# MLA scores with a 128-row last product, and a down projection in 512-column matmuls

## The chip, the cores and the metric

One core of a Trainium2 chip. The time is what the device takes for one execution of the program, in microseconds (us), the median of several runs. Inputs and outputs lie in the device's memory (HBM).

## The reference

A backbone of two layers over 512 latent tokens and 256 context tokens, 1024 features, float32. Layer 1 mixes tokens by multi-head latent attention (MLA), layer 2 by a bidirectional gated recurrence. After each comes a SwiGLU feed-forward network with 2816 inner features. RMSNorm with a shift, a scale and a gate from the conditioning vector (adaLN) stands around each part. The parts that matter here:

```
# MLA: 8 heads; a query and a key have 128 own features and 64 rotary ones, and the rotary key is shared by all heads
q = concat([q_nope, q_rope])               # 128 + 64
k = concat([k_nope, broadcast(k_rope)])    # 128 + 64
s = einsum('bhqd,bhkd->bhqk', q, k) * scale
p = softmax(s);  o = p @ v                 # latent queries see all 768 keys, context queries the 256 context keys

# feed-forward
y = (silu(a @ w1) * (a @ w3)) @ w2         # w2: 2816 -> 1024, the down projection
x = x + gate * y
```

Layer 2 computes the latent tokens alone, so its down projection is 1024 x 2816 by 2816 x 512.

## The kernel before

**Numbers in two parts.** TensorE (PE) multiplies in float32r, which keeps fewer bits than float32. Each operand is cut into a high part (a cast on ScalarE, ACT) and a low part (the rest, a subtraction on VectorE, DVE, or on GpSimd, POOL). A product is then three matmuls: high by high, high by low, low by high. `mm3` (L93 to L99) issues them for a list of terms into one PSUM output, so L97, L98 and L99 are the lines of most matmuls. A matmul is written (rows * columns of the stationary operand) and the columns of the moving operand: `128*128 128x512`.

**The order of the work.** The program is written as a flow of operations on tiles. A planner orders them on each engine by priorities and by costs and due times of its own, and puts in the semaphores. `self.at(name)` marks a part with a priority. On the chip each engine runs its list in that order; a tile pool with `bufs=n` has n places for a tag, and an operation that writes a tile waits until the place is free.

**The attention** (`mla_attend`, L427 on). For each of 8 heads, products from the latent vectors are normalised, rotated, transposed (L489) and cut (L490 to L492) into `qk_hi` and `qk_lo`. Slot 0 holds the query's own features, slot 1 the key's, and slot 2 of `qk_hi` the rotary query: its high part on partitions 0 to 63, its low part on partitions 64 to 127. The rotary keys were made before the attention, in the loop over the six token tiles at the end of `mla_in`: `rope` delivers them in both halves of a tile, so `kr_hh` (L421) has the high part twice, and `kr_lo` (L423) the low part in partitions 0 to 63 alone. A head has six query blocks of 128 queries; four (latent) take 768 keys in chunks of 512 and 256 columns, two (context) take one chunk of 256 columns. A chunk is five matmuls into one PSUM output, L514 to L518: own features high by high, high by low, low by high; rotary features against `kr_hh` over 128 rows, which adds both parts of the query; and the rotary query's high part against `kr_lo` over 64 rows. Then DVE takes the maximum of a row (`nm`, L521), ACT the exponential (L524), DVE the reciprocal of the sum and the product with it (L526, L527), PE transposes the probabilities (L530), ACT and DVE cut them (L532, L533), and `mm3` multiplies with the values. Between these PE runs the next head's projections and products for the adaLN vectors (L158, tiles of 32 columns).

**The down projection** (`ffn_down`, L758 on). The inner features come in 11 pairs of 128. In layer 2 the first six pairs' values stay on chip in two parts (`gk`); the other five are stored to HBM and loaded again (L771) and cut (`gs`, L628 and L629). For each of eight output tiles c, three weight tiles are loaded on the queue of SyncE (L82), cast on ACT (L83) and subtracted on POOL (L84), in a ring of three places, and give 22 terms. `proj_out` makes one PSUM output for each segment of tokens that it gets, one after the other, and `residual` (L557) adds it to x with the gate. Layer 1 is called with `SEGS` (512 latent and 256 context tokens), layer 2 with `HALF` (twice 256 latent tokens). `po` takes the PSUM place by width: 512 columns from `big()`, which goes round the tags L (two places) and M (one), 256 columns from the tag q (five places). The products of the up projection before it use all eight. Each finished tile of layer 2 goes to the output at once (L788).

Of the kernel before, what the change touches and what calls it, by code (L numbers as in the profile page):

```python
# [10 lines left out]
F32 = mybir.dt.float32  # L11
# [6 lines left out]
P = 128  # L18
D = 1024
# [36 lines left out]
class Kernel:  # L56
# [14 lines left out]
    # ---- weights: float32 from DRAM, cut on chip into two float32r parts whose sum is exact  # L71
    def weight(self, name, idx, c0, c1, place=None):
        """columns c0:c1 of tile idx of a weight; a tile that was fetched ahead is handed out"""
        nc = self.nc
        key = (name, idx, c0, c1)
        if key in self.ahead:
            return self.ahead.pop(key)
        src, n = self.a[name][(*idx, slice(None), slice(c0, c1))], c1 - c0
        w = self.ring.tile([P, RING], F32, tag="wf", name="wf", bufs=4)
        with self.at("w"):  # L80
            hi, lo = place or (self.ring.tile([P, RING], F32R, tag=t, name=t, bufs=3) for t in ("wh", "wl"))
            nc.sync.dma_start(out=w[:, :n], in_=src)  # L82
            nc.scalar.copy(hi[:, :n], w[:, :n])  # L83
            nc.gpsimd.tensor_sub(lo[:, :n], w[:, :n], hi[:, :n].bitcast(F32))  # L84
        return hi, lo
# [7 lines left out]
    def mm3(self, out, terms):  # L93
        """out = sum over terms of (lhs_hi + lhs_lo)^T (rhs_hi + rhs_lo) but for lo lo."""
        nc, n = self.nc, len(terms)
        for i, ((lh, ll), (rh, rl)) in enumerate(terms):
            nc.tensor.matmul(out, lhsT=lh, rhs=rh, start=(i == 0), stop=False)  # L97
            nc.tensor.matmul(out, lhsT=lh, rhs=rl, start=False, stop=False)  # L98
            nc.tensor.matmul(out, lhsT=ll, rhs=rh, start=False, stop=(i == n - 1))  # L99

    def mm3m(self, outs):
        """mm3 of several outputs, their terms taken in turn"""
        nc = self.nc
        n = len(outs[0][1])
        for i in range(n):
            for out, terms in outs:
                (lh, ll), (rh, rl) = terms[i]
                nc.tensor.matmul(out, lhsT=lh, rhs=rh, start=(i == 0), stop=False)
                nc.tensor.matmul(out, lhsT=lh, rhs=rl, start=False, stop=False)
                nc.tensor.matmul(out, lhsT=ll, rhs=rh, start=False, stop=(i == n - 1))  # L110
# [38 lines left out]
    # ---- adaLN vectors: n chunks of 128 outputs (n <= 4), both streams  # L149
# [20 lines left out]
    def norm_scale(self, l, which, ks=range(KD)):  # L170
        """w * (1 + scale): [P, KD, 2]"""
        nc = self.nc
        m0 = 8 if which == 0 else 32
        k0, n = ks[0], len(ks)
        if k0 == 0:
            self.nsc[(l, which)] = self.const.tile([P, KD, 2], F32, name=f"nsc{l}{which}")
        v0 = (VEC_N1 if which == 0 else VEC_N2) + l * KD + k0
        w = self.vec[:, v0:v0 + n].unsqueeze(2).broadcast_to([P, n, 2])
        nc.vector.scalar_tensor_tensor(self.nsc[(l, which)][:, k0:k0 + n], self.mod[l][:, m0 + k0:m0 + k0 + n, :], 1.0, w,
                                       op0=ALU.add, op1=ALU.mult)  # L180

    # ---- RMSNorm over features of x (feature-major), modulated, cut in two parts
# [13 lines left out]
    def norm_rb(self, acc, segs, pool, rb, nt):  # L196
        """1/rms of every token, on all partitions, for each segment, from the sums of squares plus D * eps"""
        nc = self.nc
        rs, rbs = [], []
        for i, (s, c0, c1) in enumerate(segs):  # L200
            n = c1 - c0
            t4 = n // P
            tp = nt()
            for t in range(t4):
                nc.tensor.transpose(tp[:, t * P:(t + 1) * P], acc[:, c0 + t * P:c0 + (t + 1) * P], self.ident)
            r = pool.tile([P, 2, LT], F32, tag=f"nr{i}", name="nr", bufs=1)
            rs.append((r, t4))
            nc.vector.tensor_reduce(r[:, 0, :t4], tp[:, :n].rearrange("p (t f) -> p t f", f=P), axis=AX.X, op=ALU.add)
            nc.gpsimd.tensor_tensor(r[:, 1, :t4], r[:, 0, :t4], self.half.broadcast_to([P, t4]), op=ALU.pow)
        for i, (r, t4) in enumerate(rs):  # L210
            dg = pool.tile([P, LT, P], F32, tag="dg", name="dg", bufs=2)
            nc.vector.tensor_tensor(dg[:, :t4], self.ident.unsqueeze(1).broadcast_to([P, t4, P]),
                                    r[:, 1, :t4].unsqueeze(2).broadcast_to([P, t4, P]), op=ALU.mult)
            o = rb(i, *segs[i][1:])
            nc.tensor.matmul(o, lhsT=self.ones, rhs=dg[:, :t4].rearrange("p t f -> p (t f)"), start=True, stop=True)
            rbs.append(o)
        return rbs

    def norm(self, l, which, x, rbs, segs, pool, a_hi, a_lo, ks=range(KD)):
        """x: the streams, feature-major"""  # L220
# [13 lines left out]
    # ---- 1/sqrt(v + eps) of small tiles, with one Newton step  # L234
# [15 lines left out]
    def rope(self, out, m, tab, pool):  # L250
        """out [P, t, 128] (both halves alike) = m*tab0 + swap(m)*tab1, m [P, t, 64]"""
# [72 lines left out]
    def mla_in(self, es, mla, a_hi, a_lo):  # L324
# [9 lines left out]
        with ExitStack() as es1:  # L334
# [13 lines left out]
            # half of the features after the other: their shifts and scales, the normed streams, the projection's weights  # L348
# [12 lines left out]
        # tables  # L361
# [19 lines left out]
        # latent projections, token-major  # L381

        def proj(ts):
            """the first tokens' products go feature tile by feature tile, as the norm delivers them"""
# [14 lines left out]
        for t in range(TT):  # L399
# [23 lines left out]
            nc.vector.tensor_sub(kr_lo[0:64, ts], tp[0:64, 5, :], kr_hh[0:64, ts].bitcast(F32))  # L423
# [3 lines left out]
    def mla_attend(self, es):  # L427
        """the heads' outputs in two parts, and the first products of them for the latent tokens"""
# [9 lines left out]
        for h in range(H):  # L438
            # queries of two heads at once; a pair's columns: k0 and k1 of the queries, k2 and keys/values, keys/values
# [12 lines left out]
            for t0 in range(0, TT, BT):  # L452
                with self.at("m_proj"):
# [14 lines left out]
                    # columns of raw: q nope 128, q rope 64, k nope 128  # L468
# [24 lines left out]
            if h == H - 1:  # L493
                # in the place of what no head needs any more
# [5 lines left out]
            with self.at("m_att" if h < H - 1 else "m_last"):  # L500
                for q0, nq, k0, k1 in ((0, 2, 0, TT), (2, 2, 0, TT), (4, 2, 4, TT)):
# [3 lines left out]
                    for qi in range(nq):  # L505
                        qs = slice((q0 + qi) * P, (q0 + qi + 1) * P)
                        sc = ps.tile([P, NT], F32, tag="sc", name="sc")
                        for c0, c1 in ((0, 512), (512, 768)):
# [9 lines left out]
                            mm(o, lhsT=qk_hi[0:64, 2, qs], rhs=kr_lo[0:64, cs], start=False, stop=True)  # L518
# [32 lines left out]
    def residual(self, x, k, pos, gate, segs, pool=None, acc=None):  # L551
        """x[k] += gate * pos, and the squares of the new x[k] into acc"""
# [49 lines left out]
    # ---- products by Strassen and Winograd's scheme: seven for a 2 x 2 of blocks, rows by columns by tokens  # L602
    def strassen_weights(self, raw, w, fs, on_dve):
        """raw: the two rows' blocks [A11 A12], [A21 A22] of w columns each. Generator of (hi, lo) of the seven
        operands in the order of use: A11, A12, S2, S1, S3, S4, A22"""
# [25 lines left out]
    def ffn(self, es, l, x, segs, acc, ps, spool=None, acc1=None):  # L631
# [10 lines left out]
        with ExitStack() as es2:  # L642
            fs = self.pool(es2, "fs")
            fop = self.pool(es2, "fop")
            # parts hi, lo of the token blocks B11, B21, B22, T1, T3, T4, T2 of features k, k + 4; B12 is in T1's place at first
# [7 lines left out]
            # T1 until it may be written: in the place of what the first pair gives  # L653
# [43 lines left out]
    def strassen_tokens(self, y, T1):  # L697
        """y: token blocks B11, B12, B21, B22, the last three replaced by T3, T4, T2"""
# [10 lines left out]
    def ffn_first(self, l, p, hn, ops, fs, ps, st):  # L709
        """a pair of feature tiles block by block, as the norm delivers the operands"""  # L710
# [47 lines left out]
    def ffn_down(self, es, l, x, segs, n, gk, gd, ps, spool, acc):  # L758
# [4 lines left out]
        for p0, p1 in chunks:  # L763
# [14 lines left out]
            for c in range(KD):  # L778
# [5 lines left out]
                with self.at("d_mm"):  # L784
                    po = self.proj_out(ps, terms, segs)
                    self.residual(x, c, po, self.mod[l][:, 40 + c, :], segs, spool if last else None, acc if last else None)
# [3 lines left out]
    def lower_bounds(self):  # L790
        """softmax of lb_logits over the two layers: p1 is this layer's bound, p0 = 1 - p1; columns [dir, head]"""
# [16 lines left out]
    def layer1(self, es, x, f_hi, f_lo, es_act):  # L808
        nc, a = self.nc, self.a
        with ExitStack() as es1:  # L810
# [4 lines left out]
            with ExitStack() as es3:  # L815
# [12 lines left out]
                # products of the heads at hand while the last one is under way  # L828
# [50 lines left out]
    def hproj(self, h, m, ps, a_hi, a_lo, segs, turn=False):  # L879
        """feature-major projection m of head h, one PSUM tile for each token segment"""  # L880
# [11 lines left out]
    def head_proj(self, h, a_hi, a_lo, hp, tmp, ps):  # L892
        nc = self.nc
        # X slots: q fb.., kf, kb, q ff..; F: f by direction (backward, forward)
# [33 lines left out]
    def head(self, h, ih, pr, oT, tmp, ps, msk, zero, won):  # L928
        nc = self.nc
        X, F, Fc, Kc, q, k0, gs = pr  # L930
        # context: keys decayed to the context's end (forward) and to its start (backward)
# [15 lines left out]
        # levels inside the blocks of 32  # L947
# [3 lines left out]
        for l in range(6):  # L951
            L = 0 if l == 0 else 1 << (l - 1)
            if l:
                # keys of even blocks run forward, of odd blocks backward; the queries the other way
# [16 lines left out]
        # blocks of 32 and 64 in a tile of 128  # L971
# [23 lines left out]
        # states at the tiles' edges  # L995
# [14 lines left out]
        # readout  # L1010
# [23 lines left out]
    def grow(self, X, T, L, tmp):  # L1034
        """From blocks of L tokens to blocks of 2L: decays of the neighbour block onto queries and keys."""
# [13 lines left out]
def pack(i):  # L1049
    """The inputs in the layouts that the kernel loads; nothing but copies."""  # L1050
    f = {k: np.asarray(v) for k, v in i.items()}

    def cols(w, n):
        """[K, n*c] -> [c, 128, K/128 * n]"""
# [27 lines left out]
    # which pairs of a block of 32 tokens meet at which level: of shapes alone  # L1082
# [3 lines left out]
    # rotary tables: of the grid's shape alone  # L1086
# [25 lines left out]
```

## Time and profile before

| | |
|---|---|
| median of 3 runs | 1897.63 us (1892.61 to 1898.05) |
| profiled execution, first to last instruction | 1898.5 us |
| its time beside the span | not listed; the runs above are other executions |
| PE busy | 1799.4 us, 95% |
| PE weight loads (PEld) busy | 1619.9 us, 85% |
| DVE, ACT, POOL busy | 1127.1, 719.3, 840.6 us |
| DMA | 188.90 MB, mean 100 GB/s |

A matmul is pipelined: its length in the profile holds its way through the array, and the next one starts long before its end. So what a matmul costs in a full stream is the distance between the starts of two neighbours, and the sum of the lengths says little.

### The profile page before, as it was taken

The page shows a single profiled execution, that of the slowest core. Times are in us where ns is not written, and L with a number is a line of the kernel's source. Part 1 is how long each engine was busy: PE and PEld are TensorE (multiplying, and loading weights), DVE is VectorE, ACT ScalarE, POOL GpSimd, SP SyncE. Part 2 cuts the span into 40 slices and gives each one's busy share as a digit, 9 for nine tenths or more (in the row PEclk, how much of TensorE's full clock was granted, in tenths as well). Part 3 has the DMA queues.
Part 4 walks back from the last instruction along what each step waited for, and adds up shares of the span by engine and source line. Part 5 has one row for each costly group of instructions (what it writes and reads, how often), then busy time and mean ns, then how long its engine had stood idle before and what let it go on. Part 6 is the DMA issues. An engine that isn't in the chain of part 4 may idle for free. (4 is left out here: it accounts for less than half of the span.)

```text
span 1898.5 us, 34179 instructions
## 1 busy us (share of the span) xinstructions
PE 1799.4 (95%) x14170; PEld 1619.9 (85%) x14170; DVE 1127.1 (59%) x1733; ACT 719.3 (38%) x1347; POOL 840.6 (44%) x568
## 2 busy tenths in 40 slices
PE   5889999999999999999999999999998899999999
PEld 3878888778799999988887889888886689899999
DVE  5566786751667777643203666565654389999400
ACT  4354555542453333332212333323232454443311
POOL 1332332214566666653443554545533553334442
PEclk8999999999999999999999999999999999999999
DMA  8311131433322223244224111212116423334531
GB/s 268 127 42 49 42 104 59 161 97 122 123 61 106 98 92 105 91 142 154 84 70 146 63 62 46 67 46 68 46 46 205 154 76 95 96 101 125 187 107 49
DMA packets 56458, 188.90 MB, mean 100 GB/s; under 512 B 6384, under 2 KB 8688, under 8 KB 56304
## 3 DMA queue, kind: packets, MB, share of 16 engines
q1 hardware_dynamic: 54144, 176.24, 28.8%
q10 hardware_dynamic: 2160, 10.49, 1.6%
q8 instruction: 111, 1.82, 0.4%
q14 instruction: 43, 0.35, 0.1%
HBM read 174.12 MB, written 12.58 MB: 98 GB/s over the span
## 5 line engine op out<-in xcount | busy, mean ns | idle before, releaser
L84 POOL TENSOR_TENSOR wl<-wf,wh 128x1024 fp32r<-128x1024 f32 (+2 forms) x130 | 288.2, 2224 | 246.1 <-ACT wh L83 245.8
L623 POOL TENSOR_TENSOR sl<-wf,sh 128x1024 fp32r<-128x1024 f32 x80 | 163.4, 2046 | 206.8 <-ACT sh L622 206.8
L99 PE MATMUL q<-op,sl 128*128 128x384 f32 (+1 forms) x700 | 215.6, 312 | 8.9 <-DVE sl L623 5.6
L97 PE MATMUL q<-op,sh 128*128 128x384 f32 (+1 forms) x700 | 216.6, 310 | 0.7 <-ACT sh L622 0.7
L98 PE MATMUL q<-op,sh 128*128 128x384 f32 (+1 forms) x700 | 216.5, 310 | 0.0
L83 ACT CAST wh<-wf 128x1024 fp32r<-128x1024 f32 (+2 forms) x130 | 122.6, 946 | 226.9 <-PE q L98 129.6
L99 PEld LDWEIGHTS q<-op,sl 128*128 128x128 f32 x700 | 130.8, 188 | 12.4 <-DVE sl L623 8.5
L97 PEld LDWEIGHTS q<-op,sh 128*128 128x128 f32 x700 | 131.8, 188 | 1.1 <-ACT sh L622 1.1
L98 PEld LDWEIGHTS q<-op,sh 128*128 128x128 f32 x700 | 131.7, 188 | 0.0
L622 ACT CAST sh<-wf 128x1024 fp32r<-128x1024 f32 x80 | 66.8, 836 | 114.0 <-PE q L98 66.4
L1043 DVE TENSOR_TENSOR X<-X,T 128x512 f32<-128x512 f32 x96 | 77.1, 845 | 52.4 <-PE lv L968 46.7
L99 PE MATMUL L<-op,sl 128*128 128x256 f32 (+1 forms) x284 | 88.6, 312 | 1.7 <-DVE sl L623 1.7
L98 PE MATMUL q<-gs,wh 128*128 128x256 f32 x320 | 90.2, 283 | 0.0
L99 PE MATMUL q<-gs,wl 128*128 128x256 f32 x320 | 90.1, 283 | 0.0
L97 PE MATMUL q<-gs,wh 128*128 128x256 f32 x320 | 90.1, 283 | 0.0
L97 PE MATMUL L<-op,sh 128*128 128x256 f32 (+1 forms) x284 | 88.1, 310 | 0.3 <-ACT sh L622 0.3
L98 PE MATMUL L<-op,sh 128*128 128x256 f32 (+1 forms) x284 | 87.9, 309 | 0.0
L958 POOL TENSOR_SCALAR km<-X 128x512 f32<-128x512 f32 x40 | 29.6, 742 | 120.2 <-DVE X L1043 77.6
L97 PE MATMUL L<-f_hi,wh 128*128 128x512 f32 (+1 forms) x232 | 79.5, 343 | 0.0
L98 PE MATMUL L<-f_lo,wh 128*128 128x512 f32 (+1 forms) x232 | 79.4, 342 | 0.0
L99 PE MATMUL L<-f_hi,wl 128*128 128x512 f32 (+1 forms) x232 | 78.9, 340 | 0.0
L611 DVE TENSOR_TENSOR sa<-wf 128x512 f32<-128x512 f32 x40 | 73.8, 1845 | 6.9 <-POOL sl L623 6.9
(468 smaller groups left out, 5643.7 us busy)
## 6 DMA issues: line engine op xcount, KB each, us to landing
wf<-in_W SPq DMA_DIRECT2D x104, 512.0 KB, 3.5
adaw<-in_ADA SPq DMA_DIRECT2D x96, 512.0 KB, 4.4
wf<-in_HW SPq DMA_DIRECT2D x32, 512.0 KB, 3.6
wf<-in_W SPq DMA_DIRECT2D x24, 384.0 KB, 3.3
gd<-s SPq DMA_DIRECT2D x10, 768.0 KB, 3.2
g<-gd ACTq DMA_DIRECT2D x10, 768.0 KB, 4.9
wf<-in_W SPq DMA_DIRECT2D x16, 320.0 KB, 3.3
wf<-in_MWO SPq DMA_DIRECT2D x8, 512.0 KB, 4.3
```

The source lines that it names most:

```text
L83: nc.scalar.copy(hi[:, :n], w[:, :n])
L84: nc.gpsimd.tensor_sub(lo[:, :n], w[:, :n], hi[:, :n].bitcast(F32))
L97: nc.tensor.matmul(out, lhsT=lh, rhs=rh, start=(i == 0), stop=False)
L98: nc.tensor.matmul(out, lhsT=lh, rhs=rl, start=False, stop=False)
L99: nc.tensor.matmul(out, lhsT=ll, rhs=rh, start=False, stop=(i == n - 1))
L611: nc.vector.tensor_add(b(sa, 1), b(r1, 0), b(r1, 1))
L622: nc.scalar.copy(hi[:, :n], s)
L623: (nc.vector if j in on_dve else nc.gpsimd).tensor_sub(lo[:, :n], s, hi[:, :n].bitcast(F32))
L958: nc.gpsimd.tensor_scalar(km.rearrange("p (m b r) -> p m b r", b=2, r=L), mix, 1.0, 0.0, op0=ALU.mult, op1=ALU.add)
L1043: nc.vector.tensor_tensor(v, v, t, op=ALU.mult)
```

## The change

Two edits, and comments are taken out, which changes no instruction. In the first, the low part of the rotary keys is kept in both halves of its tile, and the last of the five score products runs over 128 rows. Its result then also has the product of the two low parts of the rotary features. In the second, layer 2's down projection makes one PSUM output of 512 columns for the first seven output tiles; the eighth stays in two halves. Layer 1's stays as it is.

```diff
@@ mla_in
-            nc.vector.tensor_sub(kr_lo[0:64, ts], tp[0:64, 5, :], kr_hh[0:64, ts].bitcast(F32))
+            nc.vector.tensor_sub(kr_lo[:, ts], tp[:, 5, :], kr_hh[:, ts].bitcast(F32))
@@ mla_attend
                             mm(o, lhsT=qk_hi[:, 2, qs], rhs=kr_hh[:, cs], start=False, stop=False)
-                            mm(o, lhsT=qk_hi[0:64, 2, qs], rhs=kr_lo[0:64, cs], start=False, stop=True)
+                            mm(o, lhsT=qk_hi[:, 2, qs], rhs=kr_lo[:, cs], start=False, stop=True)
@@ ffn_down
                 with self.at("d_mm"):
-                    po = self.proj_out(ps, terms, segs)
-                    self.residual(x, c, po, self.mod[l][:, 40 + c, :], segs, spool if last else None, acc if last else None)
+                    sg = SEGS if l == 0 else SEGS[:1] if c < KD - 1 else HALF
+                    po = self.proj_out(ps, terms, sg)
+                    self.residual(x, c, po, self.mod[l][:, 40 + c, :], sg, spool if last else None, acc if last else None)
```

## Rows read from the trace of the kernel before

**Rows 1.** The page: header, and busy time, share of the span and instructions of each engine.
```profile
span 1898.5 us, 34179 instructions
...
PE 1799.4 (95%) x14170; PEld 1619.9 (85%) x14170; DVE 1127.1 (59%) x1733; ACT 719.3 (38%) x1347; POOL 840.6 (44%) x568
```

**Rows 2.** Busy us (count) of PE, PEld, DVE, ACT, POOL; clock; DMA; 140 to 424 us.
```profile
140.00:424.00 284.00, 277.12 (x2106) 223.51 (x2106) 202.10 (x453) 147.43 (x360) 81.47 (x90) 0.99 0.27 88
```

**Rows 3.** Timeline of PE over one block of scores (start, length, engine, line, operands, form).
```profile
303.08 0.39 PE L515 MATMUL sc<-qk_lo,qk_hi 128*128 128x512 f32 x1
...
303.54 0.39 PE L517 MATMUL sc<-kr_hh,qk_hi 128*128 128x512 f32 x1
303.86 0.50 PE L518 MATMUL sc<-kr_lo,qk_hi 64*128 64x512 f32 x1
304.29 0.38 PE L514 MATMUL sc<-qk_hi 128*128 128x256 f32 x1
304.51 0.28 PE L515 MATMUL sc<-qk_lo,qk_hi 128*128 128x256 f32 x1
...
304.75 0.28 PE L517 MATMUL sc<-kr_hh,qk_hi 128*128 128x256 f32 x1
304.95 0.38 PE L518 MATMUL sc<-kr_lo,qk_hi 64*128 64x256 f32 x1
...
305.49 0.28 PE L99 MATMUL ov<-pt_hi,v_lo 128*128 128x256 f32 x1
```

**Rows 4.** The instructions of line 518 (count, shortest, median and longest in ns, forms).
```profile
L518 PE MATMUL sc<-kr_lo,qk_hi x80: 379/383/580, 139.5 to 424.0; 64*128 64x256 f32 x48, 64*128 64x512 f32 x32
```

**Rows 5.** Waits of PE, 139 to 424 us (us in total, times, longest).
```profile
PE M L489 <- DVE qk_hi L492: 3.3, 2, 2.8
...
PE L L158 <- DMA adaw<-in_ADA: 0.2, 1, 0.2
```

**Rows 6.** Waits of DVE, 139 to 424 us.
```profile
DVE nm L521 <- PE sc L518: 30.0, 28, 2.6
DVE pt_lo L533 <- ACT pt_hi L532: 19.7, 21, 2.1
DVE rinv L526 <- ACT p L524: 14.6, 19, 2.1
...
DVE v_lo L467 <- ACT v_hi L466: 0.3, 1, 0.3
```

**Rows 7.** Timeline of PE where layer 2's down projection begins.
```profile
1767.33 0.28 PE L99 MATMUL q<-op,sl 128*128 128x256 f32 x1
1767.44 0.28 PE L97 MATMUL q<-gk,wh 128*128 128x256 f32 x1
```

**Rows 8.** Timeline of PE in layer 2's down projection, ten steps.
```profile
1820.01 0.28 PE L97 MATMUL q<-gk,wh 128*128 128x256 f32 x1
...
1821.21 0.28 PE L98 MATMUL q<-gs,wh 128*128 128x256 f32 x1
```

**Rows 9.** The instructions of line 423.
```profile
L423 DVE TENSOR_TENSOR kr_lo<-tp,kr_hh x6: 272/273/273, 94.6 to 115.3; 64x128 fp32r<-64x128 f32 x6
```

**Rows 10.** Timeline of PE in layer 1's down projection, ten steps.
```profile
949.73 0.39 PE L97 MATMUL M<-gs,wh 128*128 128x512 f32 x1
...
952.00 0.39 PE L98 MATMUL M<-gs,wh 128*128 128x512 f32 x1
```

**Rows 11.** Timeline of DVE where layer 2's down projection begins.
```profile
1789.29 1.23 DVE L629 TENSOR_TENSOR gs<-g,gs 128x1024 fp32r<-128x1024 f32 x1 [4.46 <-ACT gs L628]
```

**Rows 12.** The same view, 424 to 440 us.
```profile
424.00:440.00 16.00, 14.13 (x77) 12.10 (x77) 3.97 (x9) 2.75 (x7) 0.00 (x0) 0.79 0.14 42
```

**Rows 13.** Timeline of PE at the attention's end.
```profile
426.03 0.58 PE L97 MATMUL ov<-pt_hi,v_hi 128*128 128x256 f32 x1 [0.89 <-ACT pt_hi L532]
...
427.62 0.42 PE L97 MATMUL ov<-pt_hi,v_hi 128*128 128x256 f32 x1
...
430.61 0.41 PE L99 MATMUL ov<-pt_hi,v_lo 128*128 128x256 f32 x1
```

## The prediction

> **What bounds the kernel now.** I read the page first: the header gives a span of 1898.5 us, and TensorE (PE) is busy 95% of it, far ahead of every other engine [rows 1]. Modelled matmul ends make "busy" an upper figure, so the next question is what sets the pace of PE in the two stages that the change touches.
>
> The first is the MLA attention, from about 140 to 424 us. Its busy times by stretch show PE at 277 of 284 us and VectorE (DVE) at 202 [rows 2]. In the timeline of PE the reader is to look at the starts, not the lengths: the distance from one start to the next is what a matmul costs in a full stream. One block of scores is shown whole [rows 3]. Two steps between 128-row products of 512 columns take 303.54 - 303.08 = 0.46, so 0.23 us each. Then comes the 64-row product of L518. It starts 0.32 after its predecessor, the next product 0.43 after it, and even the one behind that 0.22 later, where the same pair of 256-column products further down the block stands 0.12 apart (304.75 - 304.51 = 0.24 for two). So the 64-row product hinders the stream on its way in, on its way out and once more behind it. There are 80 of them, 48 with 256 columns and 32 with 512 [rows 4]. PE waits for other engines only 6.5 us in this stage, in six kinds of wait [rows 5]. DVE waits much more, and for two sorts of reasons: 30.0 us for the scores (nm, the row maximum, behind L518), and 43.8 us in seven kinds of wait for ScalarE (ACT), of which the two largest and the smallest are shown [rows 6].
>
> The second is layer 2's down projection, from 1767.44 us [rows 7] to the end. PE runs through it without a gap, in 256-column products. Ten steps take 1821.21 - 1820.01 = 1.20 us, 0.120 each [rows 8].
>
> **Edit 1: 128 rows in L518.** A chunk of 512 columns costs 304.51 - 303.54 = 0.97 us from L517 to the second product after L518. As plain 128-row products the three steps are 0.23 + 0.23 + 0.12 = 0.58. That frees 0.39 us. A chunk of 256 costs 305.49 - 304.75 = 0.74, against 3 x 0.12 = 0.36, which frees 0.38 [rows 3]. For all 80 that is 32 x 0.39 + 48 x 0.38 = 30.7 us. Where a transposition or an adaLN product on a 32-column tile follows, less of the third step is to be had; I take off 5% for them: 29 us of PE time.
>
> A rule of the Trainium skill speaks against this part: TensorE: Matmul & The Clock Gate, section "Why this matters for your kernels", says that a single matmul over 32 rows takes the same time as one over 128. By that rule edit 1 would free nothing. The starts above disagree, by 0.38 to 0.39 us a product; what they look like is in TensorEngine Tiling, section "Key Properties", by which a change of the tiling mode drains the array.
>
> How much of the 29 us reaches the end depends on DVE. The score product releases the row maximum, so DVE's waits tell where the scores are late: 28 times, among 48 query blocks (8 heads, 6 blocks each) [rows 6]. There an earlier score goes straight on: 28/48 x 29 = 17 us. In the other 20 blocks DVE comes to the maximum after the scores are there; PE then runs ahead into products that need what DVE and ACT still make (the transpositions of probabilities and of queries and keys). Of those 12 us I count half, 6 us. Together 23 us. Bounds: 29 if PE's other work always covers, 12 if DVE's order binds in most blocks. DVE's budget allows the value: 202.1 busy + 43.8 waiting for ACT = 246 us, below the 284 - 23 = 261 that would be left [rows 2, 6]. What is late next is therefore the pair DVE and ACT, and PE's waits should grow from 6.5 us to about 6.5 + 29 - 23 = 12.
>
> The rest of edit 1: the subtraction for kr_lo takes 0.27 us on 64 partitions, six times [rows 9]. On 128 partitions it works on the same 128 elements a partition. Bounds: from no change to twice as long, 6 x 0.27 = 1.6 us; I take 0, since the work of one partition is the same, and it lies before the attention on an engine with gaps. The 128-row product reads the lower half of the query tile too, but the product before it (L517) already waited for that half, so no wait is added. The behaviour of the planner, which places the products by costs of its own, is not shown by any row; if its order changes, the bounds above are where I let it move the result.
>
> **Edit 2: 512 columns in the down projection.** Seven of eight output tiles have 22 x 3 = 66 products in each half. Before, 7 x 132 steps of 0.120 us [rows 8]; after, 7 x 66 of 512 columns. Layer 1's down projection has that shape: ten steps take 952.00 - 949.73 = 2.27, 0.227 each [rows 10]. 462 x (0.240 - 0.227) = 6.0 us, all on the path, since PE has no gap here and the tail (the eighth tile, in halves) stays as it is. The seven residuals become one DVE instruction each, on an engine that is nearly idle there: nothing.
>
> The Trainium skill's gap formula (TensorE: Matmul & The Clock Gate, section "Back-to-back issue gap": columns / 2.4 GHz plus 2.5 ns) would make a pair of halves 218.3 and the whole 215.8 ns, so 1.2 us instead of 6.0. The rows are longer at both widths, 120 and 227 ns, and the durations measured here are used.
>
> What can take some back is the stage's start. The last of five reloaded g tiles is split only at 1789.29 + 1.23 = 1790.5 us, 23 us after the first product [rows 7, 11]. Until then PE lives on the products of the kept and the early tiles. The ring holds three weight tiles: 20 of tile c = 0's 22 terms and 16 of c = 1's are possible, 36 x 3 x 0.227 = 24.5 us against 23.1. So it is covered, by 1.4 us; before it was 36 x 3 x 0.240 = 25.9. The outputs move from five banks (q) to three (L, M); two are open at a time, so three do. Cost between 0 and 3 us, I take 0.5. Edit 2: 5.5 us.
>
> **Sum.** 1898.5 - 23 - 5.5 = 1870.0 us for the profiled execution's span. Its time beside the span is not listed; the median of the three runs is 0.9 us below that span, so I predict 1869 us.
>
> **Rivals.**
> 1. Full return (29 + 6 us: 1863). For it: DVE and ACT have 38 us to spare on average by the budget above. Against: 20 blocks in which DVE is late already.
> 2. DVE and ACT bind (12 + 5: 1881). For it: the two waits of DVE for ACT of 19.7 and 14.6 us are links of one softmax chain, which no faster PE shortens [rows 6]. Against: the budget.
> 3. The time around L518 is not its 64 rows but the end of an accumulation, since it is the last product of its chunk, and it stays. Then only edit 2 gives: 1898 - 5.5 = 1892. Against: the down projection goes from one output to another, 1767.33 to 1767.44, in 0.11 us [rows 7]. The Trainium skill's rule on few rows, above, leads to this same case.
> 4. Slower: PE now waits in each block and its clock falls. At the end of the attention PE waited 0.89 us and then 0.41, the granted clock is 0.79 over that stretch, and 14 steps of 256 columns take 430.61 - 427.62 = 2.99, 0.214 each, the lower level of 1.2 GHz [rows 12, 13]. One such stretch loses 14 x 0.094 = 1.3 us at least. Against a gain of 28.5 it decides from 22 of the 48 blocks; with 30 of them 1869 + 39 = 1908. Against it: the clock stood at 0.99 over the whole stage [rows 2], and the waits to come are an eighth of a microsecond a block on average.
> 5. The start of the down projection runs dry: the planner finishes tile 0 before tile 1, and PE stands from 1767.4 + 20 x 3 x 0.227 = 1781 to 1790.5. That loses some 9 us: 1878.
>
> **How the numbers follow.** Forecast 0.60, rival 1 0.15, rival 2 0.14, rival 3 0.04, rival 4 0.03, rival 5 0.04. The forecast's own range is 1864 to 1875. For 8 in 10 it reaches to rivals 1 and 2, with 3 us on each side for the spread of runs: 1860 to 1884. About 0.3%, 5.7 us, is what a measurement can tell from no change: rival 3 just misses it, and with a little of the others "same" gets 0.05, slower 0.03, faster 0.92.
>
> **What would show it.** Edit 1: L518 as 128*128 in the forms, steps of 0.23 and 0.12 us through a block of scores, and the attention ending near 401 us instead of 424. DVE's wait for the scores well under 30 us, PE's own near 12. Edit 2: steps of 0.227 us to L and M from the start of the down projection, and the stage shorter by 5 to 6 us. Wrong would be: a gap left around L518 with 128 rows; PE's waits above 20 us; a clock below 0.95 in the attention; a hole in PE between 1755 and 1770 us.

## The result and the profile after

The changed kernel takes **1868.78 us** (median of 4 runs, 1863.57 to 1871.02) against 1896.51 us for the kernel before (4 runs, 1892.61 to 1898.05). The ratio is 0.9853, with a 95% interval of 0.9834 to 0.9872. The forecast was 1869. Its profiled execution took 1871.02 us, with this header and busy row, to be read against [rows 1]:

```profile
span 1869.2 us, 33246 instructions
...
PE 1762.3 (94%) x13708; PEld 1590.5 (85%) x13708; DVE 1120.9 (60%) x1726; ACT 718.9 (38%) x1347; POOL 844.1 (45%) x568
```

**The block of scores.** The timeline of PE over one block after the change (start, length, engine, line, operands, form), the answer to [rows 3]:

```profile
283.75 0.39 PE L517 MATMUL sc<-kr_hh,qk_hi 128*128 128x512 f32 x1
283.98 0.39 PE L518 MATMUL sc<-kr_lo,qk_hi 128*128 128x512 f32 x1
284.21 0.28 PE L514 MATMUL sc<-qk_hi 128*128 128x256 f32 x1
284.32 0.28 PE L515 MATMUL sc<-qk_lo,qk_hi 128*128 128x256 f32 x1
...
284.56 0.28 PE L517 MATMUL sc<-kr_hh,qk_hi 128*128 128x256 f32 x1
284.68 0.28 PE L518 MATMUL sc<-kr_lo,qk_hi 128*128 128x256 f32 x1
284.80 0.28 PE L98 MATMUL ov<-pt_lo,v_hi 128*128 128x256 f32 x1
284.92 0.28 PE L99 MATMUL ov<-pt_hi,v_lo 128*128 128x256 f32 x1
```

Look at the starts. From L517 to the second product behind L518 the chunk of 512 columns now takes 284.32 - 283.75 = 0.57 us, where it took 0.97; the chunk of 256 takes 284.92 - 284.56 = 0.36, where it took 0.74. Nothing is left around L518.

**The attention.** Its length is best read from the first and the last start of L518, since the stage begins at another moment in each execution. After the change, the instructions of line 518 (count, shortest, median and longest in ns, first and last start):

```profile
L518 PE MATMUL sc<-kr_lo,qk_hi x80: 277/283/415, 133.0 to 394.5; 128*128 128x256 f32 x48, 128*128 128x512 f32 x32
```

That is 394.5 - 133.0 = 261.5 us, against 424.0 - 139.5 = 284.5 before [rows 4]: 23.0 less. The busy times of that stretch (PE, PEld, DVE, ACT, POOL; then clock, DMA share, GB/s), the answer to [rows 2]:

```profile
133.00:395.00 262.00, 250.42 (x2112) 222.10 (x2111) 201.84 (x457) 146.86 (x360) 82.26 (x91) 0.99 0.29 97
```

DVE and ACT have the same work as before in less time, and the clock stays at 0.99, the level of 2.4 GHz. PE's waits in the stage (us in total, times, longest), first after the change, then the rows of before that do not stand in [rows 5]:

```profile
PE M L489 <- DVE qk_hi L492: 4.0, 2, 2.7
PE ov L98 <- DVE pt_lo L533: 1.9, 2, 1.4
PE sc L514 <- ACT p L524: 1.9, 3, 1.1
PE L L97 <- ACT wh L83: 1.3, 1, 1.3
PE L L158 <- DMA adaw<-in_ADA: 0.9, 2, 0.6
PE L L164 <- ACT rows L161: 0.7, 2, 0.4
PE L L97 <- DVE v_lo L467: 0.3, 1, 0.3
PE M L489 <- ACT sq L470: 0.2, 1, 0.2
```

```profile
PE sc L514 <- ACT p L524: 1.4, 2, 1.1
PE ov L98 <- DVE pt_lo L533: 0.7, 1, 0.7
PE L L164 <- ACT rows L161: 0.5, 2, 0.3
PE L L97 <- ACT wh L83: 0.4, 1, 0.4
```

They add up to 11.2 us against 6.5, 4.7 more, and no kind of wait grew by more than 1.2. DVE's waits moved the other way (after the change, answer to [rows 6]):

```profile
DVE nm L521 <- PE sc L518: 16.4, 17, 2.0
DVE pt_lo L533 <- ACT pt_hi L532: 14.4, 17, 2.1
DVE rinv L526 <- ACT p L524: 12.5, 16, 1.3
```

The wait for the scores fell from 30.0 us in 28 times to 16.4 in 17.

**The down projection.** PE's timeline from the stage's beginning to its last product, the answer to [rows 7, 8]; then the last product before the change:

```profile
1744.34 0.39 PE L97 MATMUL M<-gk,wh 128*128 128x512 f32 x1
...
1762.49 0.39 PE L97 MATMUL M<-gs,wh 128*128 128x512 f32 x1
1762.95 0.50 PE L98 MATMUL M<-gs,wh 128*128 128x512 f32 x1
...
1774.68 0.39 PE L97 MATMUL L<-gk,wh 128*128 128x512 f32 x1
...
1776.95 0.39 PE L98 MATMUL L<-gk,wh 128*128 128x512 f32 x1
...
1865.20 0.28 PE L99 MATMUL q<-gs,wl 128*128 128x256 f32 x1
```

```profile
1894.29 0.28 PE L99 MATMUL q<-gs,wl 128*128 128x256 f32 x1
```

Ten steps take 1776.95 - 1774.68 = 2.27, 0.227 each. The stage takes 1865.20 - 1744.34 = 120.86 us against 1894.29 - 1767.44 = 126.85 [rows 7], 6.0 less. The only irregular step near the start is the one of 1762.95 - 1762.49 = 0.46, which lost 0.23. Such a step stands in before_again too (0.41 us at 1779.56) and in changed_again there is none, so it need not be the edit's.

**The whole span** then adds up as below. The two stretches that no edit touches differ between executions of one and the same kernel: the changed kernel ran once more with 136.5 and 1342.8 us in the first and third row, the kernel before with 134.7 and 1340.5. In this pair they cancel.

| stretch (us) | before | after | difference |
|---|---|---|---|
| to the first L518 | 139.5 | 133.0 | -6.5 |
| attention, first to last L518 | 284.5 | 261.5 | -23.0 |
| to the down projection | 1343.4 | 1349.8 | +6.4 |
| down projection | 126.9 | 120.9 | -6.0 |
| behind the last product | 4.2 | 4.0 | -0.2 |
| span | 1898.5 | 1869.2 | -29.3 |

### The profile page after: what moved, and what is told of

Its sections match the earlier page's. It is cut to its first block, busy times and chain, and to the rows that moved or that the text cites. A ratio compares the mean times of both kernels' runs of the same rounds, so it can differ in the third digit from the quotient of the medians.

```text
span 1869.2 us, 33246 instructions
## 1 busy us (share of the span) xinstructions
PE 1762.3 (94%) x13708; PEld 1590.5 (85%) x13708; DVE 1120.9 (60%) x1726; ACT 718.9 (38%) x1347; POOL 844.1 (45%) x568
## 5 line engine op out<-in xcount | busy, mean ns | idle before, releaser
L99 PEld LDWEIGHTS q<-op,sl 128*128 128x128 f32 x700 | 130.8, 188 | 12.4 <-DVE sl L623 8.2
L557 DVE SCALAR_TENSOR_TENSOR xl<-L,mod,xl 128x512 f32<-128x512 f32 x25 | 18.7, 750 | 145.3 <-PE L L99 140.7
L622 ACT CAST sh<-sa 128x1024 fp32r<-128x1024 f32 x40 | 42.0, 1050 | 93.2 <-PE q L98 48.8
L194 POOL TENSOR_TENSOR acc<-acc,sq 128x512 f32<-128x512 f32 (+1 forms) x30 | 32.2, 1073 | 93.8 <-ACT sq L190 66.3
```

The lines of the kernel that those rows point to most:

```text
L194: (eng or nc.gpsimd).tensor_add(acc[:, c0:c1], acc[:, c0:c1], sq[:, :n])
L622: nc.scalar.copy(hi[:, :n], s)
```

## Experiments

The main theory: a product of 64 rows among products of 128 costs PE 0.38 to 0.39 us for the change of form (from 128*128 to 64*128) and back, and a part of what its removal frees is given back as waits. Against it: the cost belongs to the last product of an accumulation; or 64 rows cost by themselves; and, for the part given back, several bounds. Times are medians; a gain is (1 - ratio) times the time before in the same comparison, about 1896 us.

| kernel | us (runs) | ratio to before, 95% | gain |
|---|---|---|---|
| rows128: edit 1 alone | 1872.4 (6) | 0.9889, 0.9865 to 0.9912 | 21.0 |
| cols512: edit 2 alone | 1893.01 (12) | 0.9975, 0.9962 to 0.9989 | 4.7 |
| adjacent: 64-row products side by side | 1884.27 (6) | 0.9934, 0.9910 to 0.9958 | 12.5 |
| middle: 64-row product third in its chunk | 1898.34 (12) | 1.0014, 1.0001 to 1.0026 | -2.7 |
| wide_only: 128 rows in the wide chunks only | 1884.68 (12) | 0.9955, 0.9936 to 0.9974 | 8.5 |
| four_products: edit 1 without the fifth product | 1869.8 (6) | 0.9862, 0.9836 to 0.9888 | 26.1 |
| changed_again: the changed kernel once more | 1867.4 (6) | 0.9830, 0.9804 to 0.9856 | 32.2 |
| before_again: the kernel before once more | 1892.98 (12) | 0.9988, 0.9974 to 1.0003 | 2.3 |
| keys_only: L423 on 128 partitions alone | 1895.03 (12) | 1.0000, 0.9984 to 1.0017 | 0 |
| scale_on_act: changed, one DVE step on ACT | 1868.54 (5) | 0.9843, 0.9817 to 0.9869 | 29.8 |
| query_on_pool: changed, one DVE step on POOL | 1866.08 (5) | 0.9836, 0.9809 to 0.9863 | 31.1 |
| no_scale: changed, without L527 | 1871.42 (6) | 0.9871, 0.9845 to 0.9896 | 24.4 |

**One edit at a time.** rows128 has the first two hunks of the change, cols512 the last, keys_only the first alone.

> Edit 1 alone: the kernel before with the low rotary keys in both halves and the last score product over 128 rows. My theory (the 64-row product hinders TensorE's stream by 0.38 to 0.39 us each, and VectorE and ScalarE give back some of it): 23 us less than before, ratio 0.988, TensorE's own steps around L518 28 to 29 us shorter in all and 5 to 6 us of new waits elsewhere in the attention. The rival that a product over few rows costs no more, and the time came from elsewhere: ratio 1.000. Were part of the gain made by edit 2 only together with edit 1: less than 20 us.

> Edit 2 alone: the kernel before with seven tiles of layer 2's down projection in 512 columns. My theory (462 pairs of 0.120 us become single steps of 0.227): 6 us less, ratio 0.997, with the attention as in the kernel before. A rival by which the step is columns / 2.4 GHz plus a small fixed part: 1 us less, ratio 0.9994. This run also shows whether the first 139 us, which neither edit touches, take 6 us less in some executions than in others: if they do here without edit 1, that part of the profiled difference isn't the change's.

> The kernel before with the low part of the rotary keys in both halves of its tile (L423 on 128 partitions), the score product still over 64 rows. Theory that this subtraction costs and gives nothing: ratio 1.000 within 0.002, attention 284.5 us long, first L514 start near 137. Rival that this line's place or length brings the attention's earlier start: first L514 start at 131 to 135, and up to 4 us less in the time (0.998).

> The kernel before, once more, for the spread of its stages. In the profiles so far the first score product L514 starts at 136.7 to 137.6 us in kernels without the 128-row product, and at 131.3 to 135.2 in kernels with it. If that lead is of one execution and not of the edit, this one lies anywhere between 131 and 138; if the edit brings it, near 137. The attention's length, from the first to the last start of L518, should repeat 284.5 within 1 us by either, and the ratio 1.000 within 0.003.

Line 518 in rows128, in cols512, and in before_again:

```profile
L518 PE MATMUL sc<-kr_lo,qk_hi x80: 278/283/415, 135.0 to 397.7; 128*128 128x256 f32 x48, 128*128 128x512 f32 x32
```

```profile
L518 PE MATMUL sc<-kr_lo,qk_hi x80: 379/382/579, 138.6 to 423.9; 64*128 64x256 f32 x48, 64*128 64x512 f32 x32
```

```profile
L518 PE MATMUL sc<-kr_lo,qk_hi x80: 379/382/502, 134.7 to 417.5; 64*128 64x256 f32 x48, 64*128 64x512 f32 x32
```

With 64 rows the attention takes 284.5 (before), 285.3 (cols512), 282.8 (before_again) and 282.7 us (keys_only, 136.7 to 419.4), on the mean 283.8. With 128 rows it takes 261.5 (after), 261.8 (changed_again, 136.5 to 398.3) and 262.7 (rows128), on the mean 262.0. So single profiles of one kernel differ by 2 us here, more than the 1 us expected for before_again, and the gain is 21.8 by the means. The earlier start of the stage, which every kernel with 128 rows had shown, is not the edit's: before_again has it too, its first L514 at 132.9 us, so the 134.8 of keys_only doesn't speak for that kernel's rival. The subtraction alone changes nothing that can be measured. The ratios of the two edits multiply to 0.9889 x 0.9975 = 0.9864, inside the interval of both together. So the edits act apart, each in its own stage.

**Where the 64 rows stand.** In `adjacent` there are still 80 products of 64 rows; in the 32 blocks of two chunks the second chunk begins with its own:

```diff
+                            few = c0 > 0 and k0 == 0
+                            if few:
+                                mm(o, lhsT=qk_hi[0:64, 2, qs], rhs=kr_lo[0:64, cs], start=True, stop=False)
...
-                            mm(o, lhsT=qk_hi[0:64, 2, qs], rhs=kr_lo[0:64, cs], start=False, stop=True)
+                            if not few:
+                                mm(o, lhsT=qk_hi[0:64, 2, qs], rhs=kr_lo[0:64, cs], start=False, stop=True)
```

> Still 80 products over 64 rows, but in the 32 blocks with two chunks the second chunk begins with its 64-row product, right behind the first chunk's: 48 changes into the 64-row form and 48 out of it in place of 80 and 80. Theory of the change of form (the cost is at the change between 128 and 64 rows): 32 x 0.38 = 12 us of TensorE time freed, of which about 10 arrive: ratio 0.995. Rival, few rows cost by themselves (each 64-row product is slow): no change, ratio 1.000. Rival, the end of an accumulation costs: no change either, and the cost would stay behind the last product of the second chunk, now one over 128 rows.

In `middle` the product is the third of its chunk and L517's product ends the accumulation:

```diff
                             mm(o, lhsT=qk_hi[:, 0, qs], rhs=qk_lo[:, 1, cs], start=False, stop=False)
+                            mm(o, lhsT=qk_hi[0:64, 2, qs], rhs=kr_lo[0:64, cs], start=False, stop=False)
                             mm(o, lhsT=qk_lo[:, 0, qs], rhs=qk_hi[:, 1, cs], start=False, stop=False)
-                            mm(o, lhsT=qk_hi[:, 2, qs], rhs=kr_hh[:, cs], start=False, stop=False)
-                            mm(o, lhsT=qk_hi[0:64, 2, qs], rhs=kr_lo[0:64, cs], start=False, stop=True)
+                            mm(o, lhsT=qk_hi[:, 2, qs], rhs=kr_hh[:, cs], start=False, stop=True)
```

> Still 80 products over 64 rows, each moved from the fifth to the third place of its chunk. Theory of the change of form: the long steps move with it, from 0.32 and 0.43 (512 columns) at the chunk's end to the third and fourth product, and the time stays: ratio 1.000, 0.2 us a chunk of it either way. Rival, the end of an accumulation (its last product, the change to another output) costs: the long steps stay at the end of the chunk, and the third and fourth products take 0.23 us.

PE's timeline in adjacent (L522 and L516 have 64 rows), then in middle (L516 has):

```profile
176.12 0.39 PE L520 MATMUL sc<-kr_hh,qk_hi 128*128 128x512 f32 x1
176.44 0.50 PE L522 MATMUL sc<-kr_lo,qk_hi 64*128 64x512 f32 x1
176.78 0.28 PE L516 MATMUL sc<-kr_lo,qk_hi 64*128 64x256 f32 x1
176.99 0.38 PE L517 MATMUL sc<-qk_hi 128*128 128x256 f32 x1
177.21 0.28 PE L518 MATMUL sc<-qk_lo,qk_hi 128*128 128x256 f32 x1
```

```profile
179.35 0.40 PE L515 MATMUL sc<-qk_lo,qk_hi 128*128 128x512 f32 x1
179.67 0.50 PE L516 MATMUL sc<-kr_lo,qk_hi 64*128 64x512 f32 x1
180.10 0.50 PE L517 MATMUL sc<-qk_hi,qk_lo 128*128 128x512 f32 x1
180.44 0.40 PE L518 MATMUL sc<-kr_hh,qk_hi 128*128 128x512 f32 x1
180.67 0.28 PE L514 MATMUL sc<-qk_hi 128*128 128x256 f32 x1
```

In adjacent two 64-row products cost together what one cost: from 176.12 to 177.21 are 1.09 us, where four plain steps take 0.23 + 0.23 + 0.12 + 0.12 = 0.70, so 0.39 too much for the pair. That removes 32 x 0.39 = 12.5 us, and 12.5 (8.0 to 17.1) arrive in the times, though the planner moved some of PE's other work too. If 64 rows cost by themselves, two would cost twice. In middle the long steps moved with the product: 180.44 - 179.35 = 1.09 against 0.69 for three, again 0.40 too much, while the end of the accumulation, from L518 to the next chunk's first product, now takes a plain 0.23. Rival 3 falls by both. middle is a little slower (2.7 us, with an interval that almost reaches none). Added up from start to start, the waits left out, its score products and the one behind each chunk take 106.0 us, where the four profiles with the 64-row product last take 103.5 to 104.4. About 2 us of the loss lie there: in third place every 64-row product has another 128-row score product behind it, where at the chunk's end some have a transposition or an adaLN product, behind which less was to be had.

**How much arrives.** wide_only takes the 32 long steps of the wide chunks away and leaves 48:

```diff
+                            rows = P if c0 == 0 else 64
-                            mm(o, lhsT=qk_hi[0:64, 2, qs], rhs=kr_lo[0:64, cs], start=False, stop=True)
+                            mm(o, lhsT=qk_hi[0:rows, 2, qs], rhs=kr_lo[0:rows, cs], start=False, stop=True)
```

(L423 is on all 128 partitions here. The chunks at column 0 are the 32 of 512 columns; all 48 of 256 begin at column 512.)

> Edit 1 in the 32 chunks of 512 columns alone; the 48 of 256 columns keep their 64 rows. TensorE's own steps get 32 x 0.39 = 12.5 us shorter. Theory that what the attention gives back grows as TensorE's lead shrinks (the first part of the gain arrives whole, as it did with the 12 us of the adjacent products): 12 us less than before, ratio 0.9935. Rival, a fixed share of 0.8 arrives: 10 us less, ratio 0.9947. The two are within the interval of each other, so TensorE's steps outside L518 in the profile decide: below 1 us of new waits by the first, 2 to 3 us by the second.

four_products is rows128 without the fifth product of a chunk.

```diff
-                            mm(o, lhsT=qk_hi[:, 2, qs], rhs=kr_hh[:, cs], start=False, stop=False)
-                            mm(o, lhsT=qk_hi[:, 2, qs], rhs=kr_lo[:, cs], start=False, stop=True)
+                            mm(o, lhsT=qk_hi[:, 2, qs], rhs=kr_hh[:, cs], start=False, stop=True)
```

> Edit 1's kernel without L518: the rotary queries' product with the low part of the rotary keys is left out. That takes 32 x 0.23 + 48 x 0.12 = 13 us of TensorE's steps more than edit 1 does, with no work of VectorE or ScalarE less. Theory that TensorE still sets the pace in the attention after edit 1, with a loss of a fifth in waits: 10 us less than edit 1 alone, ratio 0.9835 of before. Rival, VectorE and ScalarE set it by then: under 4 us less, ratio 0.987 to 0.989, and TensorE's waits in the attention grow by over 9 us.

wide_only gained 8.5 us of the 32 x 0.39 = 12.5 that it was to free, between 4.9 and 12.1, so it is nearer to a share than to a full return, which lies just outside. Its engines have the order of before, and its profile decides as the expectation said: from start to start, the steps at the fifth product and behind it are 11.4 us shorter than before (55.8 against 67.2), and all other steps of the stage 2.4 longer, where the share stood for 2 to 3 and the full return for under 1. four_products takes another 32 x 0.23 + 48 x 0.12 = 13.1 us of steps from rows128, and gains 5.1 more: the ratios differ by 0.0027, and their intervals (half widths 0.0024 and 0.0026) make that 5.1 +- 6.6. This can't be told from nothing, nor from 10. Its profile is of its slowest execution (1879.48 us), so it only hints: the first score product L514 runs from 133.4 to 395.6, 262.2 us, where rows128 has 263.9, and PE's nine kinds of wait add up to 19.7 us, the largest of them this:

```profile
PE tp L529 <- DVE pt_lo L532: 3.9, 2, 2.2
```

What PE no longer does turned mostly into waiting there. The granted clock of its attention is 0.97, where the others have 0.99, and its own instructions stand in another order than in rows128, since the planner worked with other costs; so the run can't say how much of that is the engines' limit.

**What keeps the rest back?** Three kernels take work off DVE in the changed kernel. In two of them another engine gets it; no_scale has no L527.

```diff
@@ scale_on_act, L527
-                        nc.vector.tensor_scalar(p[:, ks], p[:, ks], rinv, None, op0=ALU.mult)
+                        nc.scalar.activation(p[:, ks], p[:, ks], AF.Copy, scale=rinv)
@@ query_on_pool, L480
-                    nc.vector.tensor_tensor(n3[:, :, 0, :], qw, r[:, :, 0:1].broadcast_to([P, BT, DN]), op=ALU.mult)
+                    nc.gpsimd.tensor_tensor(n3[:, :, 0, :], qw, r[:, :, 0:1].broadcast_to([P, BT, DN]), op=ALU.mult)
@@ no_scale, L527
-                        nc.vector.tensor_scalar(p[:, ks], p[:, ks], rinv, None, op0=ALU.mult)
```

> The changed kernel once more, to have it on the same chip as the two that follow and to see a second execution's profile. Ratio 0.985 to 0.987 of before. Theory that the 5.2 us of new waits in the attention belong to the order (they were 5.2 us in the run of edit 1 alone too): again 5 us here. Rival, they are chance: between 0 and 8.

> The changed kernel with the product of the exponentials and the reciprocal (L527, 48 times, 29.6 us of VectorE in the attention) on ScalarE. Theory that VectorE's order gives back 5 to 6 us of the gain: 2 to 5 us less than the changed kernel, ratio 0.983 to 0.985 of before. Rival, the chain of maximum, exponential, scaling and transposition binds by its length, in which ScalarE is the longer-loaded link now: no change, or 3 us more, ratio 0.986 to 0.988.

> The changed kernel with the scaling of the queries' own features (L480, 16 times in all, 0.65 us each, 10 us) on GpSimd, which is busy under a third of the attention. Theory of VectorE's order: 1 to 2 us less than the changed kernel. Rival, the transpositions of queries and keys (L489) wait for the end of the chain over GpSimd, which gets longer by about 0.4 us in 16 places: no change, or up to 5 us more.

> The changed kernel without the product of the probabilities with the reciprocal of their sum (L527); the division by the sum is left out. It takes 29 us of work from DVE and some 0.6 us out of the softmax chain of each block, and no other engine gets it. Theory that the length of a block's chain through DVE and ACT keeps back the 5 us that didn't arrive: PE's waits fall from 11 to under 7, the attention shortens from 261.5 to 256 to 258, the time by 4 to 6 us beyond the changed kernel (0.982). Rival that the waits are scattered among other steps (the queries' and keys' normalisation, adaLN, a DMA): the attention stays within 2 us of 261.5 and the time within 2 us of 1868.

changed_again came out at 0.9830, below the 0.985 to 0.987 expected. Its steps away from L518 add up to 223.6 us against 218.1 before, 5.5 more: again the 5 us, in the same order of instructions. None of the other three is faster: the intervals of all four overlap. The busy times of the stage in scale_on_act and in no_scale, and line 518 in no_scale:

```profile
136.00:402.00 266.00, 248.59 (x2107) 220.98 (x2106) 176.04 (x409) 177.74 (x406) 80.24 (x90) 0.99 0.28 95
```

```profile
135.00:405.00 270.00, 249.40 (x2114) 222.04 (x2113) 179.46 (x410) 149.57 (x361) 82.09 (x91) 0.99 0.27 94
```

```profile
L518 PE MATMUL sc<-kr_lo,qk_hi x80: 276/284/415, 135.4 to 405.2; 128*128 128x256 f32 x48, 128*128 128x512 f32 x32
```

DVE is busy 176 and 179 us, where the changed kernel has 201.84, and yet the attention takes 266.0 us in scale_on_act (136.0 to 402.0), 263.6 in query_on_pool (137.5 to 401.1) and 269.8 in no_scale, not less than 261.5 but more. Both theories of the last expectation fail: the stage neither became shorter nor stayed. Comparing PE's lists shows why these runs can't decide: in all three the planner has put PE's instructions into another order, with transpositions and score products in other places among the projections. A wait that was taken away and an order that costs more can't be told apart. A kernel with less work on DVE and the order of PE held fast was not tried, so what keeps back the rest stays open.

## Why the prediction was right

**The step around L518: right.** 0.39 and 0.38 us a chunk were forecast, 0.40 and 0.38 are gone, and adjacent and middle show that the change of form is the cause. By the Trainium skill's "Why this matters for your kernels" (TensorE: Matmul & The Clock Gate) a single product over few rows takes the time of a full one, and edit 1 would have freed nothing; edit 1 alone gained 21.0 us, so for a single such product in a stream of full ones the measurement decides against it. The Trainium skill's TensorEngine Tiling (Array Packing), "Key Properties", says that a change of the tiling mode drains the array; the long steps fit that, though no row shows the array itself.

**29 us freed: right.** Adding up the distances from start to start of all PE rows of the stage, the steps at L518 and behind it became 28.5 us shorter, and all others 5.2 longer: 28.5 - 5.2 = 23.3, beside the 23.0 read from L518's first and last start. That is 7% below 30.7, where 5% were taken off, and it was taken off in the right place: on the mean of four profiles with 64 rows and three with 128, a chunk of 256 columns gave 0.19 us where an adaLN product follows and 0.23 to 0.33 where a transposition does, in place of 0.38.

**23 us arriving: right in size, the reason not shown.** This profile has 23.0, the means of several 21.8, and timed alone edit 1 gained 21.0 (16.7 to 25.6): 1 to 2 us less than forecast. PE's waits were to grow to 12, they are 11.2 (12.4 in rows128, 11.2 in changed_again), and their growth of 4.7 is nearly all of the 5.2 that the other steps lost. But the 23 came from counting 28 of 48 blocks, in which DVE waited for the scores, whole and half of the rest. That split takes DVE for the engine that holds PE back in the other 20. What grew are eight small waits, 2.2 us of them for DVE, 1.8 for ACT, 0.7 for a DMA. PE has the same list of instructions in this stage in all seven profiles named above, so it can be laid step against step, and the loss doesn't lie in 20 blocks: of 1869 steps away from L518, ten grew by more than 0.2 us on the mean, the largest by 0.8, and these ten hold 5.4 of the 5.8 us that all of them lost. By the rows, four of the ten wait for DVE (2.4 us), two for ACT (1.1), and two for the DMA of an adaLN weight (1.3), which the prediction's split doesn't have. So half of 12 us was a lucky figure. That "the pair DVE and ACT" is late next fits most of these rows; that relief of DVE would bring the rest was not confirmed by three kernels, and not refuted, since they changed PE's order too.

**The clock, the planner, the subtraction: right.** The granted clock is 0.99 over the stage, before and after, so rival 4 falls. PE's list of instructions in rows128 has the order of before, so the planner moved nothing for edit 1. L423 takes 280 to 281 ns on 128 partitions where it took 272 to 273 on 64 [rows 9]: 6 x 0.008 = 0.05 us, forecast 0, and keys_only agrees.

**Edit 2: 0.5 us too little.** 5.5 were forecast: 6.0 from the steps, less 0.5 at the start. The stage became 6.0 us shorter here and 6.4 in changed_again (1741.07 to 1861.54, 120.47 us). So the steps are right, and the start costs nothing in changed_again and at most the 0.23 us of the one irregular step here. PE takes the products of two outputs by turns there, M and L, as counted, and rival 5 falls. Timed alone the edit gained 4.7 (2.1 to 7.2), which holds both. The gap formula of the Trainium skill (TensorE: Matmul & The Clock Gate, "Back-to-back issue gap"), which that section gives for isolated matmuls, made 1.2 of it; the interval excludes that.

**Where the attention ends: 394.5, not 401.** The stage began 6.5 us earlier in this execution, as it did by 4.8 in another of the kernel before. The forecast should have been given as a length.

**The sum.** 1870 was forecast for the span, 1869.2 was measured. That closeness is luck in part, since the unchanged stretches differ by -6.5 and +6.4 in this pair. So is the median of 1868.78 us beside the forecast 1869: 0.9 us were taken off for the way from the span to the time, but in all four executions of the changed kernel the time lies 1.8 us above the span (1871.02 against 1869.2 here), and the profiled one was the slowest of the four. Rival 1 (a full return, 1863) is beaten by the attention itself, where 5 to 7 of 28.5 us did not come; rival 2 (DVE and ACT bind, 1881) by 21.8 to 23.0 against its 12.

## What to carry to other kernels

Look for single matmuls of another form (fewer rows) inside a stream, and price them by the distances of starts on both sides, not by their lengths: padding to the common form takes the price away, and two such products side by side pay it once. Give the size of what arrives as a share, worked out from who waits for whom, and state lengths of stages rather than moments. Where the order of the instructions stayed the same, lay the two lists step against step: that shows the places where the gain was lost. Where a planner orders the work by costs, an experiment that takes an operation away also changes the order: compare the lists of instructions before its time is read as a verdict.

## What the runs showed of the hardware

The price is for the change of form and not for 64 rows: a second 64-row product right behind the first came for nothing more (0.39 us for the pair). Fewer columns of the stationary operand show it too. In PE's timeline of the changed kernel the adaLN product with its 32-column tile starts 172.78 - 172.57 = 0.21 us behind a product of 256 columns, where a plain step takes 0.12:

```profile
172.45 0.28 PE L517 MATMUL sc<-kr_hh,qk_hi 128*128 128x256 f32 x1
172.57 0.28 PE L518 MATMUL sc<-kr_lo,qk_hi 128*128 128x256 f32 x1
172.78 0.64 PE L158 MATMUL L<-adaw,s 128*32 128x128 f32 x14
```

In the kernel before there are 17 such places without a wait, in the changed one 23, and the median is 0.21 us in both. What remains of such changes in this kernel was not tried.

One more thing changes with the form: when the weight load (PEld) of a product starts, which brings its stationary operand. Here are the loads of L518 and of the product behind it in the block of [rows 3], then L518's load in the same block after the change, then the loads of the pair in adjacent:

```profile
303.86 0.18 PEld L518 LDWEIGHTS sc<-kr_lo,qk_hi 64*128 64x128 f32 x1 [0.35 <-issue]
304.29 0.19 PEld L514 LDWEIGHTS sc<-qk_hi 128*128 128x128 f32 x1 [0.25 <-issue]
```

```profile
283.76 0.19 PEld L518 LDWEIGHTS sc<-kr_lo,qk_hi 128*128 128x128 f32 x1
```

```profile
176.44 0.18 PEld L522 LDWEIGHTS sc<-kr_lo,qk_hi 64*128 64x128 f32 x1 [0.36 <-issue]
176.55 0.19 PEld L516 LDWEIGHTS sc<-kr_lo,qk_hi 64*128 64x128 f32 x1
```

With 128 rows the load starts at 283.76, 0.22 us ahead of its product at 283.98, so it runs beside the product before. With 64 rows it starts at 303.86, with its product, and the next one at 304.29, again with its product. In the kernel before this holds, within 3 ns, for all 80 products of 64 rows, and for those behind them that PE did not wait for. In adjacent the second 64-row product starts at 176.78, 0.23 us behind its load, and that is the one that came for nothing. So the price goes with loads that don't start ahead. Whether the late load makes the price or both have another cause, no run here tells apart.
